# A hybrid retention and attention layer: a written order of operations in place of a list scheduler

## The chip, the core and the metric

The kernel runs on one core of one Trainium2 chip. The metric is device microseconds (us) for one execution, the median of three runs. The kernel before takes 663.64 us (663.38 to 664.61). One further execution was profiled, and its trace is what the text reads.

## What is computed

The layer works on 2048 tokens of 1024 float32 channels. All of it is float32; a dense product is made from three passes over numbers that are split into a high and a low part.

```python
def reference(x, norm_w, w_in, ret_norm_w, q_norm_w, k_norm_w, sinks, rel_bias, w_out):
    h = rms_norm(x, norm_w)                                  # 2048 x 1024
    proj = h @ w_in                                          # 2048 x 2816
    rq, rk, rv, rg, sq, sk, sv, sg = split(proj)             # 256,256,512,512,512,128,128,512
    ro = retention(rotary(rq), rotary(rk), rv)               # 4 heads, chunks of 128 tokens
    ro = groupnorm(ro) * ret_norm_w * silu(rg)
    so = sliding_window_attention(sq, sk, sv, q_norm_w, k_norm_w, sinks, rel_bias)
    so = so * silu(sg)                                       # 8 heads, window of 128 tokens
    return x + concat(ro, so) @ w_out                        # 2048 x 1024
```

## The kernel before

**The dense products.** Each of four weight blocks (512, 384, 512 and 512 columns wide on TensorE, two such columns of blocks each) is multiplied by Strassen's scheme in Winograd's form: seven products in place of eight, over pairs of 128-token tiles. `weights` and `blocks` make the sums and differences on VectorE (`sum w`, `sum x`), split each operand into a high part (`hi`, a rounding copy, mostly ScalarE) and a low part (`lo`, a subtraction on VectorE), and `products` issues 12 matmuls for each product and tile pair and gathers the results in SBUF (`copy s`, `add s`, `add t`, `add r`). In the trace these matmuls are `acc<-w,x`. The blocks stand one after the other: W2 (512 wide, until 160 us), W1 (384 wide, until about 305 us), W3 (512) and W4, the output projection (512, the last 150 us).

**The small work between them.** Attention and retention stand inside W1 and W3, in small bursts of small matmuls between the dense ones:

- `turn k`: one transpose of a key tile (`m<-ident,kn`),
- `logits`: 64 small fp32 matmuls, 128 in the trace (`m<-ks,qT`), into six PSUM banks. VectorE adds the bias to them (`lg<-m,bias,nsnk`), which frees the banks,
- `values`: 72 matmuls, 144 in the trace (`m<-pT,vn`), into four banks, which ScalarE empties (`so<-m`),
- `step`: one step of the retention (`m<-qkT`, `m<-v,qk`, `m<-state,qkT`, `m<-v,sT`).

PSUM has eight banks, and all of this shares them. SBUF tiles come from 90 places of 512 columns (tag `k`) and a few others. Between stages many tiles go through DRAM (`s_dram`, `rq_dram`, `so_dram`, `planes_dram`) and back. All plain transfers are issued by one queue, SyncE's (SP in the profile), in order: one that waits for its data holds those behind it. GpSimd (POOL) issues only the 32 adding transfers (`more`).

**What sets the order.** The program is a list of 3475 operations (`Program.op`). Each has a function that issues its instructions, the tiles that it reads and writes, a rough cost for each engine that may run it, and a due time. `Program.emit` is a list scheduler that runs while the kernel is built. It keeps a clock for each engine, takes the operation that can start first (the earlier due time decides between equals), picks a free place for each new tile, and issues the operation. It has rules for TensorE's changes between kinds of matmul, for its instruction pieces (`late`, with `PIECE`, `FIRST`, `ASKED` and `LONG`) and for the SP queue. The due times are shifted by three tables of numbers (`SHIFT`, `GROUPS`, `SINGLE`). `Order.put` then binds every instruction to the one issued before it, so that no later stage of the build changes the order.

Since every operation is issued through `Engine`, all compute instructions carry one source line, L434 in the kernel before and L497 in the changed one; the text goes by the names of tiles.

Of the kernel before, what the change touches and what calls it, by code (L numbers as in the profile page):

```python
# [63 lines left out]
SHARE = {"x": 21, "raw": 70, "acc": 96, "wr": 22, "wh": 17, "att": 49, "ret": 49, "rin": 106, "gate": 20, "mix": 35, "norm": 9, "res": 73, "turned": 2, "vn": 49, "first": 5, "block": 3, "rest": 6, "split": 57}  # L64

AHEAD_OF = {"x": 5.15, "wh": 44.79, "att": 26.63}

AHEAD, SPARE, SPARED = 15.774, 5, ("raw", "wr")
# [17 lines left out]
SEM = 0.06  # L86
# [3 lines left out]
BACKLOG = 1.5  # L90

LATE = 0.7

CUTS = {"quarters": 1, "eighths": 2, "columns": 3, "bands": 4}
ENDS = {}
CHANGE, LESSER = 0.2, 0.13

PIECE, FIRST, ASKED, LONG, MORE = 256, 193, 320, 8.0, 1.0125  # L100
# [4 lines left out]
LATER, CROWD, MOST, SOONER = 2.565, 0.719, 2, 156.112  # L105
SETTLED, INSIDE = 0.8, 0.3


def change(a, b):

    return 0.0 if a == b else LESSER if 0 < a < 3 and 0 < b < 3 else CHANGE
# [30 lines left out]
class Program:  # L142
# [5 lines left out]
    def op(self, cost, go, r=(), w=(), due=0.0, table=None, label="", also=(), many=0):  # L148


        o = Op()
        due += SHIFT.get(label, 0.0)
        due = due + GROUPS.get((label, int(due // GROUP)), 0.0) + SINGLE.get(len(self.ops), 0.0)
        o.cost, o.go, o.due, o.after, o.set, o.label, o.many = cost, go, due, [], table, label, many * MORE
# [24 lines left out]
    def emit(self):  # L179
        engines = self.engines  # L180
        avail = {e: [] for e in engines}
        free = dict.fromkeys(engines, 0.0)
        port, table, bus, cut = 0.0, None, 0.0, 0
        cap = dict(CAP)
        slots = {t: [(0.0, i) for i in range(n)] for t, n in cap.items()}
        used = dict.fromkeys(SHARE, 0)
        count = len(self.ops)
        place, border, asked = 0.0, FIRST, {}

        def late(o, s, occ):  # L190

            b, wait = border, 0.0
            while b <= place + o.many:
                a = b - ASKED
                at = s + (a - place) / o.many * occ if a >= place else asked.get(b, -LONG)
                wait = max(wait, at + LONG - s - (b - place) / o.many * occ)
                b += PIECE
            return wait

        def offer(o):  # L200
            for e in o.cost:
                bisect.insort(avail[e], (o.due, o.n, o))

        for o in self.ops:
            if not o.left:
                offer(o)
        done, now = 0, 0.0
        while done < count:
            best = None
            for e, found in avail.items():  # L210
                top = None
                base = free[e]
                if e == "T" and not cut:
                    crowd = sum(o.set in CUTS and o.ready <= base for _, _, o in found[:48])
                for due, n, o in found[:48]:
                    if top is not None and top[0] <= base + 1e-9 and not e == "T":
                        break
                    occ, lat, shared = o.cost[e]
                    s = max(base, o.ready)
                    if e == "T" and o.set:  # L220
                        if cut and o.set in CUTS:
                            s = max(base, o.ready + INSIDE)
                            if change(cut, CUTS[o.set]) < CHANGE:
                                due -= SOONER
                        else:
                            s = max(base, o.ready + SETTLED)
                            if o.set in CUTS:
                                due += LATER - CROWD * min(crowd, MOST)
                    if shared and e != "Q":
                        s = max(s, port)  # L230
                    need, short, room = {}, False, 0.0
                    for b in o.new:
                        if b.ap is None:
                            need.setdefault(b.tag, []).append(b)
                    if any(due > now + AHEAD_OF.get(b.share, 1e9) for b in o.new):
                        continue
                    spare = 0
                    if e == "Q" and need:
                        if due > now + AHEAD:
                            break  # L240
                        spare = SPARE
                    for tag, bs in need.items():
                        if tag not in slots:
                            slots[tag] = [(0.0, i) for i in range(COUNTS.get(tag, SMALL))]
                        f = slots[tag]
                        if len(f) < len(bs) + (spare if tag == "k" else 0):
                            short = True
                            break
                        room = max(room, f[len(bs) - 1][0])
                        for share in {b.share for b in bs if b.share}:  # L250
                            many = used[share] + sum(b.share == share for b in bs)
                            if many > SHARE[share] - (spare if share in SPARED else 0):
                                short = True
                    if short:
                        continue
                    s, wait = max(s, room), 0.0
                    if e == "T" and border <= place + o.many:
                        s += late(o, s, occ)
                    if e == "A" and o.set and table and o.set != table:
                        wait = 1.3  # L260
                        s += 2.0
                    if top is None or s < top[0] - 1e-9 or (s < top[0] + 1e-9 and due < top[1]):
                        top = (s, due, n, o, wait, room)
                if top is not None and (best is None or top[:3] < best[0][:3]):
                    best = top, e
            if best is None:
                self.stuck(avail, used, slots)
            (s, _, _, o, wait, room), e = best
            occ, lat, shared = o.cost[e]
            free_before = free[e]  # L270
            for e2 in o.cost:
                a = avail[e2]
                a.pop(bisect.bisect_left(a, (o.due, o.n)))
# [6 lines left out]
            if e == "Q":  # L280
                occ, lat, more = o.cost[e]
                bus = max(bus, s) + occ
                free[e] = max(s + more, bus - BACKLOG)
                o.end = bus + lat
            else:
                if wait:
                    s = s - 2.0 + wait
                if e == "A" and o.set:
                    table = o.set
                free[e] = s + occ  # L290
                o.end = s + lat
                if shared:
                    port = s + occ
                if e == "T":
                    s = max(free_before, o.ready, room) if o.set else s
                    s += change(cut, CUTS.get(o.set, 0))
                    cut = ENDS.get(o.set, CUTS.get(o.set, 0))
                    s += late(o, s, occ)
                    while border <= place + o.many:
                        border += PIECE  # L300
                    a = border - ASKED
                    while a <= place + o.many:
                        asked[a + ASKED] = s + max(a - place, 0) / max(o.many, 1) * occ if a >= place else asked.get(a + ASKED, s)
                        a += PIECE
                    place += o.many
                    free[e] = s + occ
                    o.end = s + lat
            o.seen = free[e]
            if e == "T" and o.set is None:
                now = max(now, o.due)  # L310
            o.go(engines[e])
            done += 1
            if LOG is not None:
                LOG.append((e, s, free[e], o))
            for b in o.bufs:
                b.left -= 1
                b.end = max(b.end, o.end)
                if not b.left and b.tag:
                    bisect.insort(slots[b.tag], (b.end + SEM, b.slot))
                    if b.share:  # L320
# [1493 lines left out]
```

## Time and profile before

| | us |
|---|---|
| median of three runs (lowest to highest) | 663.64 (663.38 to 664.61) |
| the profiled execution, its own time | 662.82 |
| its span, first to last instruction | 661.0 |
| TensorE (PE) busy in the span | 654.1 |
| TensorE weight loads (PEld) busy | 560.3 |
| VectorE (DVE) busy | 573.0 |
| ScalarE (ACT) busy | 466.4 |

The clock granted to TensorE was full throughout. In a row of the chain of waits the first number is the start in us, the second the length, then the engine and what it worked on; "issue" is time in which an engine waited for nothing that the profile shows. In a row of the timeline the part in brackets is idle time before the row and what ended it. A busy PE is not PE at its peak, since the ends of matmuls are modelled; so the text reads pauses of TensorE from the starts of neighbouring rows.

### The profile page before, as it was taken

Reading aid. Unit: us, or ns where it says so; the run is one execution under the profiler, and the core shown is the slowest. Engines: PE = TensorE matmul, PEld = TensorE weight load, DVE = VectorE, ACT = ScalarE, POOL = GpSimd, SP = SyncE. Lnnn points to the kernel's source line nnn. Section 1 sums busy time; section 2 is a strip of 40 time slices with the busy share of each in tenths; the row PEclk is TensorE's granted clock in tenths of the full one; section 3 lists DMA queues with packets and bytes.
Section 4 is the critical chain, followed back from the end, with each engine's and each line's share of the span. In section 5 each row is a group of like instructions: output and inputs, shape, how many; then the busy total and the mean of one; then the engine's idle time right before and its main releaser. Section 6 shows DMA issues by size and latency. Waiting matters only on the chain.

```text
span 661.0 us, 16187 instructions
## 1 busy us (share of the span) xinstructions
PE 654.1 (99%) x5926; PEld 560.3 (85%) x5926; DVE 573.0 (87%) x1328; ACT 466.4 (71%) x1140; POOL 43.5 (7%) x71
## 2 busy tenths in 40 slices
PE   9999999999999999999999999999999999999997
PEld 7888888888999999998878888888888888888886
DVE  5999985988788988799997999999999999975452
ACT  6774569958698767686988889898999675544000
POOL 0000000022300000000000000000000111133320
PEclk9999999999999999999999999999999999999999
DMA  8967369999899699699988969899999989279862
GB/s 303 389 210 249 113 200 302 367 315 310 220 253 299 189 261 288 239 331 289 298 213 259 291 168 296 247 271 272 269 277 271 230 170 234 76 116 203 191 160 96
DMA packets 153568, 160.85 MB, mean 243 GB/s; under 512 B 62096, under 2 KB 96016, under 8 KB 153488
## 3 DMA queue, kind: packets, MB, share of 16 engines
q1 hardware_dynamic: 148736, 151.43, 77.8%
q0 software_dynamic: 4608, 8.39, 8.3%
q8 instruction: 46, 0.75, 0.5%
q14 instruction: 34, 0.28, 0.1%
q10 hardware_dynamic: 144, 0.00, 0.0%
HBM read 97.58 MB, written 49.61 MB: 223 GB/s over the span
## 4 chain that ended last, share of the span: by engine, by line
PE 96%; DMA 2%; issue 0%; ACT 0%; DVE 0%; SPq 0%; POOLq 0%
PE acc L434 86%; PE m L434 10%; DMA x<-s_dram 1%; DMA x<-in_xfirst 1%; DMA rq_dram<-r 0%; SPq L434 0%; ACT x L434 0%; ACT w L434 0%; DVE x L434 0%; DVE lg L434 0%; DVE t L434 0%; DVE nm L434 0%; POOLq L434 0%
## 5 line engine op out<-in xcount | busy, mean ns | idle before, releaser
L434 PE MATMUL acc<-w,x 128*128 128x512 f32 (+1 forms) x2700 | 585.3, 377 | 0.7 <-ACT x L434 0.5
L434 PEld LDWEIGHTS acc<-w,x 128*128 128x128 f32 x2700 | 493.6, 188 | 84.6 <-issue 4.1
L434 DVE TENSOR_TENSOR x<-x 128x512 fp32r<-128x512 f32 (+2 forms) x213 | 138.5, 673 | 8.5 <-ACT x L434 8.3
L434 ACT ACTIVATE x<-x 128x512 fp32r<-128x512 f32 (+1 forms) x181 | 107.8, 620 | 42.5 <-DVE x L434 18.7
L434 DVE TENSOR_TENSOR w<-w 128x512 fp32r<-128x512 f32 (+3 forms) x96 | 61.0, 656 | 3.3 <-ACT w L434 3.1
L434 DVE TENSOR_TENSOR s<-acc,s 128x512 f32<-128x512 f32 (+1 forms) x64 | 41.6, 651 | 21.0 <-PE acc L434 20.7
L434 ACT ACTIVATE lg<-lg,nm 128x160 f32<-128x160 f32 x128 | 53.1, 418 | 7.2 <-DVE nm L434 7.1
L434 DVE SCALAR_TENSOR_TENSOR w<-w,nw_sb 128x512 fp32r<-128x512 f32 (+3 forms) x72 | 50.0, 715 | 5.1 <-ACT w L434 4.7
L434 ACT ACTIVATE w<-w 128x512 fp32r<-128x512 f32 (+1 forms) x72 | 41.7, 608 | 18.0 <-PE acc L434 9.2
L434 DVE CUSTOM_DVE_ANT_0 lg<-m,bias,nsnk 128x160 f32<-128x160 f32 x128 | 40.5, 375 | 1.5 <-PE m L434 1.5
L434 DVE TENSOR_TENSOR t<-acc,t 128x512 f32<-128x512 f32 (+2 forms) x33 | 20.8, 636 | 18.5 <-PE acc L434 18.3
L434 DVE TENSOR_TENSOR r<-acc,t 128x512 f32<-128x512 f32 (+1 forms) x32 | 20.9, 652 | 16.5 <-PE acc L434 14.0
L434 POOL DMA_DIRECT2D c<-in_xtok x8 | 7.2, 1103 | 372.4 <-DVE x L434 343.4
L434 ACT ACTIVATE w<-w,nw_sb 128x512 fp32r<-128x512 f32 (+4 forms) x41 | 26.3, 674 | 3.7 <-PE acc L434 3.1
L434 ACT ACTIVATE s<-acc 128x512 f32<-128x512 f32 (+1 forms) x32 | 18.2, 570 | 14.3 <-PE acc L434 13.7
L434 DVE STREAM_TRANSPOSE pT<-lg 128x640 f32<-128x640 f32 x32 | 25.8, 823 | 0.3 <-ACT lg L434 0.3
L434 ACT ACTIVATE ro<-ro,nmu,rg 128x128 f32<-128x128 f32 x64 | 25.3, 483 | 0.1
L434 ACT ACTIVATE c<-acc 128x512 f32<-128x512 f32 (+1 forms) x32 | 18.3, 571 | 8.7 <-PE acc L434 7.7
L434 ACT ACTIVATION_READ_ACCUMULATOR lg<-lg,nm 128x1 f32 x128 | 24.3, 189 | 0.0
L434 ACT ACTIVATE x<-go 128x512 fp32r<-128x512 f32 x26 | 15.9, 626 | 10.2 <-PE acc L434 4.3
L434 DVE TENSOR_TENSOR t<-acc,s 128x512 f32<-128x512 f32 (+1 forms) x32 | 20.7, 649 | 2.6 <-PE acc L434 2.4
L434 PE MATMUL m<-pT,vn 32*64 32x128 f32 (+1 forms) x1152 | 20.6, 285 | 0.9 <-issue 0.9
(146 smaller groups left out, 594.9 us busy)
## 6 DMA issues: line engine op xcount, KB each, us to landing
x<-in_xt SPq DMA_DIRECT2D x76, 256.0 KB, 4.9
planes_dram<-apart SPq DMA_DIRECT2D x48, 256.0 KB, 3.9
x<-s_dram SPq DMA_DIRECT2D x46, 256.0 KB, 4.4
w<-in_w_in SPq DMA_DIRECT2D x40, 256.0 KB, 5.3
xk<-in_xtok SPq DMA_DIRECT2D x32, 256.0 KB, 4.1
s_dram<-x SPq DMA_DIRECT2D x23, 256.0 KB, 3.8
w<-in_w_out SPq DMA_DIRECT2D x20, 256.0 KB, 4.0
vn<-aq_dram SPq DMA_DIRECT2D x8, 576.0 KB, 5.4
```

Source lines behind the costliest of these rows:

```text
L434: return lambda *a, **k: self.order.put(op(*a, **k))
```

## The change

The scheduler goes, and with it its rules, the shares of tiles, and the three tables of shifts. In its place stand three tables: `ORDER`, the 3475 operations as numbers in the order in which they are issued; `PLACES`, the place of each new tile, in turn; and `CHOICE`, the engine of the 18 operations that two engines could run. `emit` reads them. The operations are the same, with the same instructions, the same number of places, and the same eight banks.

```diff
     def emit(self):
-        engines = self.engines
-        avail = {e: [] for e in engines}
-        free = dict.fromkeys(engines, 0.0)
...
-        done, now = 0, 0.0
-        while done < count:
-            best = None
-            for e, found in avail.items():
...
-            o.go(engines[e])
...
+        places = iter(PLACES)
+        for n in ORDER:
+            o = self.ops[n]
             for b in o.new:
                 if b.ap is None:
-                    b.slot = slots[b.tag].pop(0)[1]
-                    if b.share:
-                        used[b.share] += 1
+                    b.slot = next(places)
                     b.ap = self.alloc(b)
...
+            o.go(self.engines[CHOICE.get(n) or next(iter(o.cost))])
+
+
+ORDER = (
+    0, 1, 2, 3, 11, 378, 379, 15, 384, 18, 389, 21, 394, 13, 380, 12, 14, 399, 382, 383, 400, 115, 401, 402, 381, 403,
...
+)
+PLACES = (
+    0, 0, 1, 2, 3, 4, 5, 6, 7, 8, 9, 10, 11, 12, 1, 2, 13, 3, 4, 14, 15, 16, 17, 18, 19, 20, 21, 22, 23, 24, 25, 26,
...
+)
+CHOICE = {380: "V", 382: "A", 38: "A", 39: "V", 36: "A", 37: "V", 866: "A", 865: "A", 864: "V", 867: "A", 2189: "A", 2188: "A", 2187: "V", 2190: "A", 2912: "V", 2909: "A", 2910: "A", 2911: "A"}
```

What the tables do to the engines' own orders is seen at three places.

**TensorE in W1.** The first rows are of the kernel before, from its first logits to the first values and on to the next logits and values.

```order
L434 MATMUL m<-ks,qT 32x160 x64
L434 MATMUL acc<-w,x 128x384 x33
L434 MATMUL m<-ident,kn 128x128
L434 MATMUL acc<-w,x 128x384 x51
L434 MATMUL m<-pT,vn 64x128 x32
L434 MATMUL m<-pT,vn 64x256 x8
L434 MATMUL m<-pT,vn 64x128 x32
L434 MATMUL acc<-w,x 128x384 x21
L434 MATMUL m<-ident,kn 128x128
L434 MATMUL acc<-w,x 128x384 x24
L434 MATMUL m<-ks,qT 32x160 x64
```

The same in the changed kernel, and behind it the second values and the third logits, and the third values and the fourth logits.

```order
L497 MATMUL m<-ks,qT 32x160 x64
L497 MATMUL acc<-w,x 128x384 x36
L497 MATMUL m<-ident,kn 128x128
L497 MATMUL acc<-w,x 128x384 x30
L497 MATMUL m<-ident,kn 128x128
L497 MATMUL acc<-w,x 128x384 x54
L497 MATMUL m<-pT,vn 64x128 x32
L497 MATMUL m<-pT,vn 64x256 x8
L497 MATMUL m<-pT,vn 64x128 x32
L497 MATMUL acc<-w,x 128x384 x24
L497 MATMUL m<-ks,qT 32x160 x64
```

```order
L497 MATMUL m<-pT,vn 64x128 x32
L497 MATMUL acc<-w,x 128x384 x15
L497 MATMUL m<-ks,qT 32x160 x64
...
L497 MATMUL m<-pT,vn 64x128 x32
L497 MATMUL acc<-w,x 128x384 x12
L497 MATMUL m<-ks,qT 32x160 x64
```

Between the first logits and the first values stand 120 dense matmuls now, 84 before. From values to the next logits there were 45 before; now there are 24, and at the next two such places 15 and 12.

**VectorE and TensorE after logits.** This is the VectorE queue of the kernel before after its fifth logits, up to the bias of the first banks.

```order
L434 TENSOR_TENSOR qn<-s,fac_89 128x512
L434 SCALAR_TENSOR_TENSOR w<-w,nw_sb 128x384 x2
L434 TENSOR_TENSOR r<-acc,t 128x384
L434 SCALAR_TENSOR_TENSOR w<-w,nw_sb 128x384 x2
L434 TENSOR_TENSOR x<-x 128x512
L434 ISA lg,nm<-m,bias,nsnk 128x160
```

In the changed kernel the tightest such place is on TensorE in W3: six dense matmuls and then a key transpose, which needs a bank that the bias frees.

```order
L497 MATMUL m<-pT,vn 64x128 x32
L497 MATMUL acc<-w,x 128x512 x36
L497 MATMUL m<-ks,qT 32x160 x64
L497 MATMUL acc<-w,x 128x512 x6
L497 MATMUL m<-ident,kn 128x128
L497 MATMUL acc<-w,x 128x512 x18
```

VectorE's queue there:

```order
L497 TENSOR_TENSOR qk<-tcos,tsin 128x8x32
L497 TENSOR_TENSOR qk<-tsin,tcos 128x8x32
L497 SCALAR_TENSOR_TENSOR w<-w,nw_sb 128x512
L497 TENSOR_TENSOR x<-x 128x512
L497 ISA lg,nm<-m,bias,nsnk 128x160
```

Two weight splits, an addition from PSUM and two more splits stood between the query's scaling and the bias before. Now two rotary sums, a weight sum and one split stand ahead of it.

**SyncE at the end.** The last rows of the queue before, and then of the changed one: `out` is the result, and c, r, s and t name its four kinds of block.

```order
L434 DMA out<-s 128x512 x2
L434 DMA out<-r 128x512
L434 DMA out<-s 128x512
L434 DMA out<-r 128x512
L434 DMA out<-s 128x512
L434 DMA out<-r 128x512
L434 DMA out<-t 128x512 x7
L434 DMA out<-t 128x384
L434 DMA out<-t 128x128
```

```order
L497 DMA out<-t 128x512
L497 DMA out<-s 128x512 x2
L497 DMA out<-t 128x512
L497 DMA out<-r 128x512 x2
L497 DMA out<-t 128x512 x3
L497 DMA out<-s 128x512 x2
L497 DMA out<-t 128x512
L497 DMA out<-r 128x512
L497 DMA out<-t 128x512
L497 DMA out<-t 128x384
L497 DMA out<-t 128x128
```

The blocks of kinds r and s, which were stored as they came, are partly stored between the last t blocks now.

At the start, the changed kernel's ScalarE runs a one-element copy first (`once`), which loads its table before any data has arrived, and VectorE, not ScalarE, makes the high part of the first 256 columns of `x`.

More of the change, by code (lines that the diff above doesn't have):

```diff
@@ L151, in op @@
         o = Op()
-        due += SHIFT.get(label, 0.0)
-        due = due + GROUPS.get((label, int(due // GROUP)), 0.0) + SINGLE.get(len(self.ops), 0.0)
-        o.cost, o.go, o.due, o.after, o.set, o.label, o.many = cost, go, due, [], table, label, many * MORE
+        o.cost, o.go, o.due, o.after, o.set, o.label, o.many = cost, go, due, [], table, label, many
         o.n, o.left, o.ready, o.end, o.seen, o.by = len(self.ops), 0, 0.0, 0.0, 0.0, None
@@ L179, in emit @@
     def emit(self):
-        engines = self.engines
-        avail = {e: [] for e in engines}
-        free = dict.fromkeys(engines, 0.0)
[L183 to L206, printed above, removed]
-        done, now = 0, 0.0
-        while done < count:
-            best = None
-            for e, found in avail.items():
[L211 to L273, printed above, removed]
@@ L274, in emit @@
+        places = iter(PLACES)
+        for n in ORDER:
+            o = self.ops[n]
             for b in o.new:
                 if b.ap is None:
-                    b.slot = slots[b.tag].pop(0)[1]
-                    if b.share:
-                        used[b.share] += 1
+                    b.slot = next(places)
                     b.ap = self.alloc(b)
[L280 to L307, printed above, removed]
@@ L308, in emit @@
-            o.seen = free[e]
-            if e == "T" and o.set is None:
-                now = max(now, o.due)
-            o.go(engines[e])
[L312 to L320, printed above, removed]
-                        used[b.share] -= 1
@@ L322, in emit @@
-            for d in o.after:
-                d.left -= 1
-                same = len(d.cost) == 1 and e in d.cost and e in ("T", "A", "Q") and not o.label.startswith("load")
-                t = o.seen if same and e != "Q" else o.end + SEM
-                if e == "Q" and now > 0:
-                    t += LATE
-                if t > d.ready:
-                    d.ready, d.by = t, o
-                if not d.left:
-                    offer(d)
-        self.time = max(free.values())
-    def stuck(self, avail, used, slots):
-        lines = [f"no operation can go: {used} { {t: len(f) for t, f in slots.items()} }"]
-        for e, found in avail.items():
-            for due, _, o in found[:4]:
-                lines.append(f"{e} {due:.1f} {o.label} needs {[(b.name, b.share) for b in o.new if b.ap is None]}")
-        raise RuntimeError("\n".join(lines))
@@ L342 @@
-LOG = None
-SHIFT = {"store ": -0.52, "square qk": -0.13, "step": -2.98, "normalise": 3.92, "lo x": -0.99, "add res": 2.35, "hi w": 1.91, "turn by dma": -5.0, "turn gated": -4.54, "load turned": 3.81, "gate": -2.87, "silu": -4.4, "sum w": 0.6, "lo w": -0.18, "sum x": -3.26, "load x": -0.14, "hi x": -0.78, "qn": 4.14, "rotary": 0.48, "bias": -0.38, "exp": 1.1, "turn weights": -1.07, "load w": 0.01, "apart": -1.33, "scale w": -4.44, "state": 0.75, "add s": 0.64, "add t": 4.54, "add r": -1.77, "more": -5.0, "copy s": -0.87, "load go": 0.06, "so": 6.55, "sum qk": 0.02, "stats": 1.22, "scale first": -2}
+            o.go(self.engines[CHOICE.get(n) or next(iter(o.cost))])
```

19 lines of the change are left out of this document (1 added, 18 removed), and 231 rows, old and new, of tables (ORDER, PLACES).

## The prediction

> **What bounds the kernel now.** I read the page first, then the chain of waits in order of time, then the timeline at each place where the chain leaves TensorE.
>
> ```profile
> span 661.0 us, 16187 instructions
> PE 654.1 (99%) x5926; PEld 560.3 (85%) x5926; DVE 573.0 (87%) x1328; ACT 466.4 (71%) x1140; POOL 43.5 (7%) x71
> ...
> PE 96%; DMA 2%; issue 0%; ACT 0%; DVE 0%; SPq 0%; POOLq 0%
> ```
>
> TensorE bounds it: 96% of the chain. The change leaves TensorE's matmuls as they are, so it can win only the time in which TensorE pauses, and the chain shows how little that is. In each of its rows stand the start, the length and the work.
>
> ```profile
> 1.68 4.08 DMA x<-in_xfirst
> ...
> 6.25 155.35 PE acc L434 x688
> 161.60 0.11 PE m L434
> ...
> 191.14 2.24 PE m L434 x124
> 193.38 0.89 issue
> 194.27 0.48 PE m L434 x15
> ...
> 216.87 2.46 PE m L434 x138
> 219.33 3.32 PE acc L434 x18
> ...
> 225.37 2.33 PE m L434 x128
> ...
> 239.46 2.57 PE m L434 x139
> ...
> 255.60 10.60 PE acc L434 x60
> ...
> 294.12 2.46 PE m L434 x138
> ...
> 482.05 43.55 PE acc L434 x192
> ...
> 526.04 131.30 PE acc L434 x588
> ...
> 657.37 0.29 DVE t L434
> ```
>
> The paces are the unit of all that follows. A 512-wide matmul takes 43.55 / 192 = 0.227 us and a 384-wide one 10.60 / 60 = 0.177 us (0.174 without its share of a changeover). A key transpose adds 0.11 us, logits 2.33 us, values 2.46 us. What the order decides is four pauses.
>
> *The hole in the second burst, 193.38.* These values took 2.24 + 0.89 + 0.48 = 3.61 us, against 2.46 us at 294.12: 1.15 us lost, with no semaphore behind it ("issue"). The transfers in that stretch, 191.0 to 193.4 us, hold this row, which the stretch of the same queue before it, 185 to 191 us, does not have:
>
> ```profile
> q8 instruction: 1, 0.02, 3.4%
> ```
>
> For the whole run the page has 46 such packets, 0.75 MB:
>
> ```profile
> q8 instruction: 46, 0.75, 0.5%
> ```
>
> TensorE's two rows count 2 x 5926 = 11852 instructions, so a packet is 11852 / 46, some 256 of them, 16 KB. One packet of instructions came while the burst was running, and TensorE stood until it was there. That is my reading; the profile names no cause. The logits (256 instructions with their weight loads) and the values (288) each use a whole packet or more in under 2.5 us, while 256 instructions of dense matmuls last 128 x 0.174 = 22 us.
>
> *The late bank, 282.26.*
>
> ```profile
> 277.35 2.40 PE L434 MATMUL m<-ks,qT 64*32 64x160 f32 x128
> 279.69 1.84 PE L434 MATMUL acc<-w,x 128*128 128x384 f32 x9
> 282.26 0.30 PE L434 MATMUL m<-ident,kn 128*128 128x128 f32 x1 [0.73 <-DVE nm L434]
> ```
>
> Nine matmuls and the changeover (18 took 3.32 at 219.33, so 0.19 over their pace) are 9 x 0.174 + 0.1 = 1.67 us, so the transpose was due at 281.36: 0.9 us lost. It waited for a bank that VectorE's bias frees. VectorE's rows say why the bias was late:
>
> ```profile
> 277.43 0.69 DVE L434 TENSOR_TENSOR qn<-s,fac 128x512 f32<-128x512 f32 x1 [1.50 <-DMA so_dram<-so]
> ...
> 281.42 0.38 DVE L434 CUSTOM_DVE_ANT_0 lg<-m,bias,nsnk 128x160 f32<-128x160 f32 x1
> 281.73 0.08 DVE L434 DVE_READ_ACCUMULATOR2_ANT nm<- 128x1 f32 x1
> 281.73 0.38 DVE L434 CUSTOM_DVE_ANT_0 lg<-m,bias,nsnk 128x160 f32<-128x160 f32 x1
> ```
>
> VectorE stood 1.50 us for a transfer, then worked off the six operations ahead of the bias without a gap, and began the bias 281.42 - 279.69 = 1.73 us after the logits were done. From its start to the transpose pass 282.26 - 281.42 = 0.84 us, two biases and the signal. So the place could bear 1.67 - 0.84 = 0.83 us, and 1.73 us late gave the pause of 0.9.
>
> *The late transpose pair, 337.08.* After a lone transpose the next matmul starts 0.03 us later (222.49 and 222.52 below); here it starts 0.36 us later. 0.33 us lost.
>
> ```profile
> 222.49 0.27 PE L434 MATMUL m<-ident,kn 128*128 128x128 f32 x1
> 222.52 2.85 PE L434 MATMUL acc<-w,x 128*128 128x384 f32 x15
> ...
> 337.08 0.27 PE L434 MATMUL m<-ident,kn 128*128 128x128 f32 x1
> 337.44 1.17 PE L434 MATMUL acc<-w,x 128*128 128x512 f32 x4
> ```
>
> *The opening.* TensorE's unbroken work begins at 6.25, after the transfer that lands at 1.68 + 4.08 = 5.76.
>
> **The change part by part.** Against the profiled execution, 662.82 us (span 661.0 and 1.8 around it); the median of the runs shown, 663.64, is 0.82 above it.
>
> The first three pauses are 1.15 + 0.90 + 0.33 = 2.38 us. Does the new order remove them? *The hole*: 120 dense matmuls stand between the first logits and the first values, where 84 stood, so the burst begins elsewhere within its 256 instructions; whether a hole comes is a matter of that place. Bounds: 1.15 won, or nothing. I take it as won, since the other seven values bursts before had no such row (216.87 is one of them). *The late bank*: VectorE now has rotary sums, a weight sum and one split ahead of the bias at its tightest place, not six operations behind a wait for a transfer. Bounds 0.9 won or nothing; I take it as won. *The transpose pair*: the same, 0.33.
>
> *The opening* stays: the first three transfers are issued in the same order, so the second half of `x` lands at 5.76 and TensorE runs from 6.25. The earlier table load moves this row off ScalarE's start:
>
> ```profile
> 3.35 1.28 ACT L434 ACT_TABLE_LOAD   x1 [3.35 <-DMA nw_sb<-in_nw]
> ```
>
> It could bring the first two matmuls forward, but those behind them wait for the landing. Bounds 0 to 0.4 won; I take 0.
> ```profile
> L434 ACT ACTIVATE x<-x 128x512 fp32r<-128x512 f32 (+1 forms) x181 | 107.8, 620 | 42.5 <-DVE x L434 18.7
> ...
> L434 ACT ACTIVATE w<-w,nw_sb 128x512 fp32r<-128x512 f32 (+4 forms) x41 | 26.3, 674 | 3.7 <-PE acc L434 3.1
> ```
>
> The moved engine choices (a net three copies from VectorE to ScalarE) lie under dense work and cost nothing; without that cover each is some 0.67 us, by the second of these rows. Transposes are as many as before, 0.11 us each, in two groups fewer: 0.
>
> *New waits.* Values fill four banks and logits need six of eight, so logits wait until ScalarE has copied the values out.
>
> ```profile
> 219.30 1.47 ACT L434 ACTIVATE so<-m 128x128 f32<-128x128 f32 x8 [1.85 <-PE m L434]
> 242.62 1.47 ACT L434 ACTIVATE so<-m 128x128 f32<-128x128 f32 x8 [1.18 <-PE acc L434]
> ```
>
> The copy takes 1.47 us and ends 1.44 us after the values at 219.33, 2.06 us after those of 239.46 + 2.57 = 242.03. The crowded places give it 24, 15 and 12 dense matmuls: 4.2, 2.6 and 2.1 us. At 12 the spare time is 0.0 to 0.65 us, at 15 it is 0.5 to 1.2, less a split of `x` (0.62, by the first of those rows) that stands between the two halves of the copy. So any lateness of ScalarE shows there. The same places bring 288 + 24 to 48 + 256 instructions in 7 to 9 us, more than two packets, where the tightest before had 33 matmuls between. Bounds for the three together: 0, or the hole of 1.15 and half a microsecond of waiting at each, 4.95. I take 0.4, near the lower end, since the closest bursts of the kernel before (values that end at 219.33, logits at 225.37) ran without a pause. *The six matmuls before the transpose in W3* last 6 x 0.227 = 1.36 us, less the same 0.84 from the bias to the transpose: VectorE may be 0.5 us late. Bounds 0 to the 0.9 seen at 282; I take 0.1.
>
> *The end.* SP now stores r and s blocks between the last t blocks. Behind the second t of the group of three stand s, s, t, r, t: with the last two of the group seven wide stores, 7 x 262 KB = 1.84 MB, ahead of the two narrow ones that end the run.
>
> ```profile
> GB/s 303 389 210 249 113 200 302 367 315 310 220 253 299 189 261 288 239 331 289 298 213 259 291 168 296 247 271 272 269 277 271 230 170 234 76 116 203 191 160 96
> ...
> out<-s SPq DMA_DIRECT2D x8, 256.0 KB, 4.4
> ...
> out<-t SPq DMA_DIRECT2D x7, 256.0 KB, 2.0
> ```
>
> At the best slice's 389 GB/s they take 4.7 us, at a middling 250 GB/s 7.4 us; t blocks come every 12 x 0.227 = 2.7 us, so about 7 us are there. Bounds: 0, or the 2.4 us by which a store among others lands later than one alone; I take 0.15.
>
> Sum: 662.82 - 2.38 + 0.4 + 0.1 + 0.15 = 661.1 for an execution like the profiled one; 0.82 above it, **661.9 us** for the median.
>
> [...]
>
> **The rivals.**
>
> *All clears* (0.13): the pauses go and nothing comes for them: 663.64 - 2.38 = 661.3, or 660.9 if the opening gains its 0.4. For it: between two uses by TensorE, VectorE's queue adds up to less than TensorE's stretch at the places that I summed. Against: the tight places above.
>
> *The pauses only move* (0.13): other transfers land late, VectorE is behind at another logits, and some 2.4 us come back: 663.6. For it: each pause came from a time that the order does not set, the landing of a packet or a transfer.
>
> *The hole is not the order's* (0.06): instructions are fetched in time, and what stopped TensorE at 193.38 stops it again: 663.64 - 0.9 - 0.33 + 0.4 = 662.8.
>
> *The crowded bursts starve* (0.13), the slower side: at the three places where logits follow values after 24, 15 and 12 matmuls, instruction packets come too late twice, once in each burst, 2 x 1.15 each: 663.64 - 2.38 + 6.9 = 668.2. It decides from 3.7 us in all, 1.25 at each place; below 2.4 us there is still a gain. For it: nothing before was that dense. Against: of all bursts before only one had a hole.
>
> **How the numbers follow.** The forecast has 0.55, and its own range is 660.7 to 663.0. A difference under 0.2%, 1.3 us, counts as no change, since runs of this kernel differ by about that. So 662.3 is the bound of faster: of the forecast 0.43 lie below it and 0.12 above, and all of "all clears": 0.56 faster. Of the pauses that move 0.10 are within, 0.03 slower; the hole that stays is within; 0.28 in all. Slower: 0.13 + 0.03 = 0.16. The range of 8 in 10 takes "all clears" on its low side and the moved pauses and half-starved bursts on its high side: 660.4 to 664.8.
>
> **What would show it.** In the changed kernel: no "issue" row inside the first values; no pause before a transpose with VectorE as releaser; the three pairs of values and close logits in W1 without a gap; dense work from about 6.2 us on; a last store that lands, as before, 3.3 us after the last addition. I am wrong if TensorE's work from 6.25 to its last matmul is not near 649 us (657.34 - 6.25 = 651.1 before), or if the end after it is longer than 4.5 us.

## The result, and the profile after

The changed kernel takes 660.58 us in the median (660.05 to 661.31), the kernel before 664.13 us in the runs beside it: a ratio of 0.9944, with a 95% interval of 0.9928 to 0.9959. That is 3.55 us less. The forecast was 661.9 us, 1.74 us less than the 663.64 us then known, so the sign is right and the gain is twice the one forecast. The time lies inside the range of 8 in 10, 660.4 to 664.8 us, and just below the forecast's own, 660.7 to 663.0. Two executions of later rounds, of 1097.63 and 1690.89 us, were disturbed, and the ranges below leave them out.

The two profiled executions show less than that. The span fell from 661.0 to 659.4 us, and the executions' own times from 662.82 to 661.31 us, which is 1.5 us. The first lies below all six timed runs of its kernel, the second is the longest of its six. So there are two questions: whether the 1.5 us came from the places that the prediction named, and where the other 2 us are.

The page of the changed kernel, with the span, the busy time by engine and the shares of the chain of waits:

```profile
span 659.4 us, 16114 instructions
PE 654.1 (99%) x5926; PEld 560.4 (85%) x5926; DVE 575.2 (87%) x1325; ACT 464.5 (70%) x1143; POOL 43.5 (7%) x71
...
PE 98%; DMA 1%; issue 0%; SPq 0%; ACT 0%; DVE 0%; POOLq 0%
```

Its chain of waits, each row with the start, the length and the work:

```profile
1.68 4.16 DMA x<-in_xfirst
...
6.33 160.55 PE acc L497 x718
...
199.13 2.46 PE m L497 x138
201.59 4.37 PE acc L497 x24
205.96 2.36 PE m L497 x128
...
223.06 2.81 PE acc L497 x15
...
245.78 2.29 PE acc L497 x12
248.07 2.33 PE m L497 x128
...
332.17 1.61 PE acc L497 x6
333.77 0.11 PE m L497
...
435.96 3.02 PE m L497 x118
438.98 0.59 issue
439.58 0.59 PE m L497 x10
...
656.16 0.29 DVE t L497
```

All the places of the prediction can be read here. The first values last 2.46 us without an "issue" row inside. The three crowded gaps of 24, 15 and 12 matmuls last 4.37, 2.81 and 2.29 us, as long as their matmuls, and logits follow at once. No transpose waits for VectorE, and the six matmuls before the transpose in W3 are followed by it directly. Dense work begins at 6.33 us (6.25 before), and TensorE's work from there to its last matmul takes 656.14 - 6.33 = 649.8 us (651.1 before; the prediction asked for about 649). The run ends 659.4 - 656.45 = 2.95 us after the last addition (661.0 - 657.66 = 3.34 before). One pause is new: a retention step, which else takes 3.25 us, takes 3.02 + 0.59 + 0.59 = 4.20 us, with an "issue" row inside. That is 0.95 us.

### The profile page after: what moved, and what is told of

Same layout as the page of the kernel before. It is cut to its first block, busy times and chain, and to the rows that moved or that the text cites. A ratio compares the mean times of both kernels' runs of the same rounds, so it can differ in the third digit from the quotient of the medians.

```text
span 659.4 us, 16114 instructions
## 1 busy us (share of the span) xinstructions
PE 654.1 (99%) x5926; PEld 560.4 (85%) x5926; DVE 575.2 (87%) x1325; ACT 464.5 (70%) x1143; POOL 43.5 (7%) x71
## 4 chain that ended last, share of the span: by engine, by line
PE 98%; DMA 1%; issue 0%; SPq 0%; ACT 0%; DVE 0%; POOLq 0%
PE acc L497 88%; PE m L497 10%; DMA x<-in_xfirst 1%; SPq L497 0%; ACT x L497 0%; DVE t L497 0%; POOLq L497 0%
## 5 line engine op out<-in xcount | busy, mean ns | idle before, releaser
L497 DVE TENSOR_TENSOR x<-x 128x512 fp32r<-128x512 f32 (+2 forms) x213 | 139.8, 677 | 13.8 <-ACT x L497 13.6
L497 ACT ACTIVATE w<-w,nw_sb 128x512 fp32r<-128x512 f32 (+4 forms) x44 | 29.1, 674 | 8.8 <-DVE w L497 4.1
L497 ACT ACTIVATE ro<-m 64x256 f32<-64x256 f32 (+2 forms) x51 | 19.6, 390 | 6.1 <-PE m L497 5.0
```

What stands on the lines that cost most here:

```text
L497: return lambda *a, **k: self.order.put(op(*a, **k))
```

## The experiments

"The kernel before" as a table means its own order of operations and places, written into the changed kernel's ORDER and PLACES; each engine then executes the same instructions as before, and single operations can be exchanged.

**Second profiles.** Both kernels were run again without an edit.

> The kernel before, unchanged, to get a second profile of it and more times. Theory A (instructions arrive late at random places): the pause with no releaser at 193.38 (0.89 us in the chain, 1.15 us in all) is gone or stands at another place in this profile, while the two pauses before transposes (0.9 us near 282, 0.33 us near 337) are there again; the runs scatter over 2 us as before, 663.4 to 665.9, by the number of such pauses, and an execution that lies at 664.1 shows two or three of them and not one. Rival B (the order itself makes that pause): it stands at 193.4 again with the same length, and the scatter comes from somewhere else, such as the end.

Measured: 663.27 us (661.54 to 666.60, 12 runs), against 663.80 us for the kernel before beside it. The chain of this second profile of the kernel before:

```profile
193.48 1.42 issue
...
554.70 8.03 DMA go<-turned_dram
...
564.25 93.12 PE acc L434 x418
```

and from its timeline VectorE's and TensorE's rows at the place of the "late bank":

```profile
276.58 0.69 DVE L434 TENSOR_TENSOR qn<-s,fac 128x512 f32<-128x512 f32 x1
...
281.94 0.27 PE L434 MATMUL m<-ident,kn 128*128 128x128 f32 x1
```

The hole in the values stands at the same place, 0.53 us longer. So theory A was wrong that its place is chance. The pause of 0.9 us at 282 is gone: VectorE did not wait for a transfer before qn, and TensorE came 0.5 us later because of the longer hole. Instead TensorE lost some 0.6 us around 564.25, where VectorE's split of x waited for a transfer that took 8.03 us. The sum of the pauses is that of the first profile within 0.1 us (1.7 + 0.05 + 0.6 for 1.15 + 0.9 + 0.33), but only the hole is the same.

> The changed kernel, unchanged, to get a second profile and more times. Theory A (instructions arrive late at random): the pause of 0.95 us at 438.98 is gone or elsewhere, and the execution takes 660.1 to 660.7 us where it has none. Rival B (the new order makes that pause): it is at 439 again, and all executions carry it. Both expect a median near 660.6.

Measured: 660.01 us (659.66 to 661.09, 5 runs). The pause at 439 is gone, and the third crowded gap has one, in the midst of the logits:

```profile
248.11 1.51 PE m L497 x76
249.62 0.42 issue
250.04 1.28 PE m L497 x52
```

These logits take 3.21 us instead of 2.33. So the changed kernel had one hole of 0.9 us in both profiles, at two places. Both profiled executions are the longest of their series (661.31 us of 660.05 to 661.31, and 661.09 of 659.66 to 661.09), so the executions that were not profiled may have less of it; no run tells.

**The place within the packets.** 

```diff
-        for n in WARM:
+        for n in WARM[:3]:
             e.matmul(pw()[:, 0:n], zero.broadcast_to([P, P]), zero.broadcast_to([P, n]), start=True, stop=True)
+        for n in range(38):
+            e.matmul(pw()[0:32, 0:16], zero.broadcast_to([P, 32]), zero.broadcast_to([P, 16]), start=True, stop=True)
```

> The changed kernel with the matmuls on zeros at the start cut into more pieces (three of 256 columns and 38 of 16 columns instead of five), so that every later TensorE instruction stands 144 places later within the packets of 256; the same order of everything else. [...] Theory A (pauses are instructions that come late): some 3 to 5 pauses of about 1 us without a releaser, inside or near the bursts of logits and values, where there was one; 662 to 665 us, most likely 663.5. Rival B (the pauses have nothing to do with instruction packets): no new pause, and 660.6 us within 0.5.

Measured: 670.18 us (668.42 to 676.16, 6 runs), 10.2 us more than the changed kernel beside it. How long ahead of its need a packet is asked for no run shows, so the number of 3 to 5 pauses was the author's estimate. The chain:

```profile
205.76 1.61 issue
...
234.51 0.69 issue
...
255.94 0.15 issue
...
259.37 1.51 issue
```

Four new pauses without a releaser stand in the bursts or right behind them. At each of them the trace has a packet of instructions that had landed 1.3 to 1.6 us before TensorE went on; at the holes of the other profiles it is 1.3 to 1.5 us. Apart from the start, nothing but the place of the instructions within their packets had been moved, so theory B falls: late instructions make these holes. Their place says the same. Counted over all of TensorE's instructions in the trace, each of the 15 such holes, in the 11 profiles of this document that have one, ends 193 instructions behind a multiple of 256: in the first profile of the kernel before after 2241 = 8 x 256 + 193, in that of the changed kernel after 9665 = 37 x 256 + 193. There the rules of the kernel before (`PIECE` 256, `FIRST` 193) let a new packet begin. From the first transpose (170.92 us here, 166.72 in the changed kernel's first profile) to that at 505 us (514.15 and 505.20) this run took 4.75 us more. The 4.2 us ahead of it were lost at the start, which I had not foreseen (see the last section).

> The kernel before with its order unchanged, and at the start six matmuls on zeros of 16 columns in place of one of 128, so that every later TensorE instruction stands 20 places later within the packets of 256. In both profiles of the kernel before, TensorE stood inside the values burst at 193.4 until 1.4 to 1.5 us after a packet of instructions had landed. Theory A (that packet makes the pause, the prediction's term of 1.15 us): the pause at 193.4 is gone or much shorter, and the median lies about 1 us below the kernel before. Rival B (something else in the order makes it): it stands where it was, within 0.3 us of its length, and the median is the same.

The edit is the same with `WARM[:4]` and `range(6)`. Measured: 662.17 us (660.42 to 665.41, 12 runs) against 662.64 us, ratio 0.9987 (0.9967 to 1.0007): by the times undecided. The timeline of its profile decides for the hole, whose values had 1.15 to 1.7 us more in every profile of the kernel before with its instructions in place:

```profile
193.13 2.53 PE L434 MATMUL m<-pT,vn 32*64 32x128 f32 x144
```

2.53 us, all in one row: the hole is gone with 20 places. This execution lost 2 us at the start again, and 0.7 us near 565.

**The pauses one by one.** First the late bank, with `1622` the two biases, `1343` the addition of r, and the rest the operations that stood between them, the splits on VectorE among them:

```diff
-    ... 1343, 928, 2184, 931, 929, 1344, 932, 1767, 1345, 1079, 1080, 1082, 1622, ...
+    ... 1343, 1622, 928, 2184, 931, 929, 1344, 932, 1767, 1345, 1079, 1080, 1082, ...
```

> The kernel before, its own order written out as a table, with one exchange: the two biases that free the bank for the key transpose at 282.26 go right behind the addition of r at 279.10 on VectorE, ahead of two splits of w and one of x. Nothing else is moved. Theory A (the term late bank of the prediction, 0.9 us, is real and can be won alone): the transpose comes at about 281.4 without a wait, and the median is 0.9 us below that of the kernel before. Rival B (pauses only move): the two splits and the split of x are 0.7 us later, TensorE waits for one of these instead, or for the later logits, and the median is within 0.3 us of the kernel before.

Measured: 664.42 us (662.85 to 666.10, 12 runs) against 663.80 us, ratio 1.0003 (0.9987 to 1.0019). Its timeline:

```profile
280.34 0.38 DVE L497 CUSTOM_DVE_ANT_0 lg<-m,bias,nsnk 128x160 f32<-128x160 f32 x1 [0.56 <-PE m L497]
...
281.83 0.27 PE L497 MATMUL m<-ident,kn 128*128 128x128 f32 x1
...
338.03 2.29 PE L497 MATMUL acc<-w,x 128*128 128x512 f32 x9 [0.68 <-DVE nm L497]
```

The bias begins right behind the logits and the transpose comes without a wait, though qn had waited 1.15 us for its transfer. But nothing is won: the pause behind the transpose near 337 is 0.9 us, where it had been 0.33. That is rival B, the pauses move.

Then all three, with the shift by 20 places, this exchange and the same for the biases at 335 (`1698` and `1700` ahead of `1731` and `2235`):

> The kernel before with all three of the prediction's pauses attacked and nothing else: the shift by 20 places, the first two biases at 282 ahead of a split of w and one of x, and the first four biases at 335 ahead of a key's rotary and a sum on VectorE. Theory A (the prediction's sum): the three pauses add up, 1.15 + 0.90 + 0.33 = 2.38 us below the kernel before, about 661.4. Theory C (in the kernel before, VectorE and ScalarE are level with TensorE at many places, so that a pause removed at one of them is met at the next, and landings that vary from run to run show up in full): less than half of it is won, 663 us or more, new waits on VectorE or on transfers stand elsewhere, and the runs still scatter over more than 2.5 us.

Measured: 664.23 us (660.74 to 665.90, 12 runs) against 662.64 us, ratio 1.0013 (0.9996 to 1.0029). The three pauses are gone. In the profile the matmul behind the transpose of W3 starts at 336.17 us, where the first profile of the kernel before has 337.44, 1.3 us earlier, though it had come 0.6 us later to its first transpose (162.08 for 161.44 us). Then it is lost:

```profile
336.17 3.68 PE L497 MATMUL acc<-w,x 128*128 128x512 f32 x15
...
429.58 10.86 PE L497 MATMUL acc<-w,x 128*128 128x512 f32 x44 [0.39 <-DVE w L497]
...
565.80 14.45 PE L497 MATMUL acc<-w,x 128*128 128x512 f32 x62 [0.83 <-DVE x L497]
```

TensorE waits for VectorE's split of w, which was not late in the profiles of the kernel before, and for the x near 565, as in the second of those profiles. That is what theory C says, and its number is met: the three edits did not win the sum of 2.38 us.

**The place near 565.** The expectation of the next run says that TensorE waited there in four of five profiles of this order; it was three. The exchange, with `2882` the store on SP:

```diff
-    2871, ... 2867, ... 3196, ... 2882, ... 3153
+    2871, 2882, ... 2867, ... 3196, ... 3153
```

> The kernel before, its own order as a table, with one exchange on SP's queue alone: the store of a piece of planes that its data let go at 535.3, and that SP issued only at 546.05 because it stood behind a load that waited for a buffer until 545.2, goes right behind the store of the piece before it, at about 540. Everything that comes of it (a transposed read, two sums and a split of x at 562.9 to 564.2, on which TensorE waited 0.6 to 1.0 us near 565 in four of five profiles of this order) is earlier by up to some us. Theory C (this chain of two transfers has no room in the kernel before, and its landings make a good part of the scatter): no wait near 565, the median 0.5 to 1.5 us below the kernel before, and the runs scatter over less than 3 us where the kernel before scattered over 5 to 6. Theory A (the three pauses of the prediction are the difference, the rest is chance): the median within 0.4 us of the kernel before, the same scatter.

Measured: 663.25 us (661.72 to 664.82, 12 runs) against 664.14 us (661.97 to 668.50, 29 runs), ratio 0.9996 (0.9981 to 1.0010). From its timeline, SP's issues and VectorE's sum:

```profile
539.58 1.05 SPq L497 DMA_DIRECT2D planes_dram<-apart  x2
...
551.01 3.25 SPq L497 DMA_DIRECT2D go<-turned_dram  x4
...
563.26 0.69 DVE L497 TENSOR_TENSOR x<-go,so 128x512 f32<-128x512 f32 x1 [0.66 <-DMA go<-turned_dram]
```

Against the second profile of the kernel before, the store goes 6 us earlier, and it doesn't help: the next link, four loads of go, is issued 0.9 us earlier and lands later. TensorE still waited there, 0.2 us, though it came 0.6 us later itself; a second late packet, in the values at 242 us, had held it 0.6 us. The runs scatter over 3.1 us, where less than 3 was expected. Theory C had the wrong link. What the loads meet there, the view of transfers shows for the stretch from 551 to 563 us (bytes of one issue and median us from issue to landing), first in this run:

```profile
out<-c SPq DMA_DIRECT2D x3, 256.0 KB, 2.8
c<-in_xtok POOLq DMA_DIRECT2D x1, 256.0 KB, 12.2
go<-turned_dram SPq DMA_DIRECT2D x4, 64.0 KB, 11.0
```

and then in the second profile of the changed kernel:

```profile
go<-turned_dram SPq DMA_DIRECT2D x4, 64.0 KB, 3.8
out<-c SPq DMA_DIRECT2D x1, 256.0 KB
```

The windows of the two (length, granted clock, share of the 16 DMA engines that is busy, above 1 where packets overlap, and GB/s), this run first and the changed kernel behind it:

```profile
557.00:560.00 3.00, 1.00 1.18 83
560.00:563.00 3.00, 1.00 1.08 276
```

```profile
557.00:560.00 3.00, 1.00 0.01 3
```

In the old order two or three stores and one or two gathers by POOL share the transfer engines with these loads, which take 6.1 to 11.0 us in four profiles of it; in the new order the engines are empty by 557 us, with a busy share of 0.00 to 0.01, and the loads take 3.6 to 3.8 us. No run moved these stores alone, so that they make the delay is read from the profiles and not shown.

All four edits together, the shift from five small matmuls behind the five wide ones:

> The kernel before with the exchange of the store and with the three edits of the run that attacked the prediction's three pauses; this time the shift by 20 places comes from five small matmuls behind the five wide ones at the start, so that the opening stays. In that earlier run TensorE was about 1.9 us ahead after the third pause and lost it again at 430 (0.56 us, VectorE's split of w) and at 565 (1.0 us). Theory C: the gain at 565 is kept now, and what was lost at 430 and later before 565 stays lost; about 661.0 us, 660.3 to 662.3, 1.5 to 3 us below the kernel before. Theory A (the sum of the prediction, 2.38 us, was reached in the chip's runs and only covered by the 565 place): 2.4 us and more below the kernel before.

Measured: 662.78 us (661.56 to 665.61, 12 runs) against 664.14 us, 1.4 us less in the medians; ratio 0.9988 (0.9969 to 1.0006). In its profile TensorE was 1.7 us ahead of the first profile of the kernel before at 336, and 0.4 us at the end. Neither theory met its number; it is nearer to C.

**Margins.** Extra work on VectorE at the same 51 places in both kernels:

```diff
+            if n in MORE:
+                for _ in range(4):
+                    self.engines["V"].memset(self.more(), 0.0)
             o.go(self.engines[CHOICE.get(n) or next(iter(o.cost))])
```

> The kernel before, its order unchanged, with extra work that nobody needs: ahead of each of 51 operations of VectorE, spread evenly over the program by number, four memsets of 128 x 64, some 0.45 us together by estimate. From the profiles of before, the time by which each of these 51 operations could be late without TensorE having to wait falls short of 0.45 us by 4.3 us in sum; for the changed kernel the same sum is 0.1 us. Theory C (the kernel before has no margin, the changed one has): 2 to 5 us slower, 666 to 669 us, with more waits on VectorE. Theory A (only the three pauses tell the kernels apart, margins don't matter): less than 1 us slower, and as much as in the changed kernel with the same extra work.

> The changed kernel with the same extra work ahead of the same 51 operations. Theory C (margins): at most 0.5 us slower than without it, 660.0 to 660.9 us, no wait of TensorE on VectorE, and runs that scatter no more than before. Theory A (margins don't matter): as much slower as the kernel before with the same work.

Measured: 681.00 us (679.36 to 683.13) for the kernel before, 18.4 us more than without; 671.95 us (670.58 to 674.15) for the changed kernel, 11 to 12 us more than its two medians without. Theory C's numbers, 2 to 5 us and at most 0.5 us, were both missed, and TensorE waits for VectorE in the changed kernel too. The memsets of one tile started 0.19 us apart, so four take 0.65 us of VectorE and not the 0.45 of the author's estimate, and by these times that is more than the changed kernel bears as well. The dose of the next two runs was chosen after this, two memsets, `range(2)`:

> The kernel before with half of the extra work on VectorE: two memsets of 128 x 64 ahead of each of the 51 operations. In the trace of the earlier run memsets start 0.19 us apart and four of them cost VectorE 0.65 us, so two cost 0.27 us. By the profiles of before, the 51 operations fall short of 0.27 us by 2.0 to 2.3 us in sum; by the profiles of the changed kernel by nothing. With four memsets both kernels lost more than twice such sums (18 us and 11 us), since lateness is carried on to the next operations. Theory C (margins): 3 to 7 us slower than the kernel before. Theory A (margins don't matter): the same loss as in the changed kernel with this work.

> The changed kernel with the same two memsets ahead of the same 51 operations. Theory C (margins): 0 to 2 us slower than without them, 660.3 to 662.3 us, at most half of what the kernel before loses by them. Theory A: as much slower as the kernel before.

Measured: 668.38 us (667.28 to 669.56, 6 runs) for the kernel before, 4.2 us more than the 664.14 us without; 661.03 us (660.10 to 662.99, 12 runs) for the changed kernel, 0.5 to 1.0 us more than its two medians without. Those are from other rounds; beside it the kernel before was 3.1 us slower, where it had been 3.55 and 3.8. The waits of TensorE (us in total, times, longest), the kernel before with the extra work:

```profile
PE acc L501 <- DVE more L501: 0.7, 1, 0.7
PE m L501 <- ACT so L501: 0.6, 1, 0.6
...
PE acc L501 <- DVE w L501: 0.5, 1, 0.5
PE m L501 <- DVE nm L501: 0.3, 1, 0.3
PE acc L501 <- DVE x L501: 0.2, 1, 0.2
```

and the changed kernel with it (the first row is the start of the program):

```profile
PE m L501 <- PEq L1869: 0.8, 1, 0.8
PE acc L501 <- ACT ro L501: 0.4, 1, 0.4
```

The same 13.8 us of work (51 x 0.27) makes TensorE wait for VectorE at four groups of places in the one kernel (the last, 0.2 us for x, stands in its second profile without the work too) and at none in the other. This is the clearest difference between the two.

Not all of the 4.2 us need be margin. TensorE's first dense rows, of the kernel before without the extra work and with it:

```profile
5.45 7.92 PE L434 MATMUL acc<-w,x 128*128 128x512 f32 x32 [0.50 <-ACT x L434]
```

```profile
5.47 7.91 PE L501 MATMUL acc<-w,x 128*128 128x512 f32 x26 [0.51 <-ACT x L501]
```

Six matmuls less in the same time are 1.4 us, lost ahead of the first memset at 39.1 us (see the last section). That execution took 668.47 us; how many of the six lost as much is not known. Without it some 3 us are left, against 0.5 to 1.0.

The traces say the same. Going back from each start on TensorE through what it needs and through the order on each engine, one can estimate by how much every VectorE operation could be later without TensorE having to wait. In the two profiles of the kernel before, 8 to 10 in 100 of these operations could not be 0.27 us late; in the two of the changed kernel, fewer than 1 in 100.

## Why the prediction was right, and too small

- *The hole, 1.15 us won.* It is gone from its place, and its cause is the one that was read from the rows: the two shifts moved and made holes with the order unchanged. But it was not won whole. The changed kernel has a hole of 0.9 us in both profiles, at 439 or at 249.6. In these two executions 0.2 to 0.3 us of the 1.15 was won.
- *The late bank, 0.90, and the transpose pair, 0.33.* Both are gone. The step that counted them as fixed prices to be added failed: in the second profile of the kernel before the first is not there and the second is 0.06 us, while 0.6 us stand near 565. What is nearly the same in the two is the sum. That each pause hides the lateness of something further on is what the single edits bear out: the pause came back near 337, at 430 and near 565.
- *The opening, 0.* Right: 6.33 for 6.25, held by the landing at 1.68 + 4.16 = 5.84.
- *The crowded gaps, 0.4.* 0 in the first profile, 0.9 in the second, at the gap of 12 matmuls. About right. The copy of so, the other suspect there, held nothing up.
- *The six matmuls in W3, 0.1, and the stores at the end, 0.15.* Neither cost anything; the end is 0.4 us shorter.
- *The sum,* 661.1 for an execution like the profiled one, met 661.31, and this is luck in part: its terms for new waits and for the end come to 0.65 us of loss, and 0.64 us was measured, but as a hole of 0.95 us at a place that it had not named, an opening 0.08 us later and an end 0.39 us shorter.
- *The step that failed* is the one that carried the sum to the median: "0.82 above it". It took the distance between the profiled execution and the median as the same in both kernels. Measured, the median lies 1.3 us above the profiled execution in the kernel before and 0.7 us below it in the changed one. That is the missing 2 us.

For the difference between executions the margin is the cause that the runs support best: a delay of 0.27 us at 51 places costs the kernel before 3 to 4.2 us and the changed kernel about 1. Landings of transfers and of instructions vary from one execution to the next (in the two profiles of the kernel before the loads of go near 551 us took 6.1 and 8.8 us in the median, and the hole 1.15 and 1.7 us), and in its profiles the kernel before lets some of this through to TensorE. Some 90 executions of it lie between 661.3 and 668.5 us; the 11 of the unedited changed kernel between 659.66 and 661.31. That the margin makes the missing 2 us is argued from this and not shown. Two other causes were seen and not set apart: a slow start, which cost 1.4 us in one of the six profiles of the old order with its start unedited and nothing in four of the changed kernel, and the hole, which the old order has in all six and twice in one. What stays open is which delays fill the longer executions of the kernel before. Its two profiled executions took 662.8 us each, and none above 664 was profiled.

Of the rivals, *the pauses only move* is what happens when the kernel before is mended at single places, but not in the changed kernel. *All clears* lay nearest in its number, at 661.3, but not in its mechanism, since a new hole came. *The crowded bursts starve* did not come to pass, though it is near: it is what the shift by 144 places does to this order. *The hole is not the order's* is out. In the first profiles of both kernels the packets of the long dense stretches, up to 161 us and from 506 us on, landed 27.07 us and more ahead of their need; in the bursts up to 1.6 us of waiting stand in the chain for one packet.

## What to carry to other kernels

Before summing up pauses on the bound engine, work out by how much the engines behind it could be late; where that is near zero, a pause removed can be met again some places further on, as here at 430 (0.39 us) and 565 (0.83 us). Take a second profile of the same kernel before pricing pauses, and count as fixed only those that stand in both. To learn whether an order has margin, put the same small extra work into both orders, in a dose near the margin that the trace shows.

## What the runs showed of the hardware

*Packets of instructions were late in bursts.* TensorE went on 1.2 to 1.6 us after the landing of the packet that it stood for, in every such hole (1.39 us in the first profile of the kernel before, 1.26 in that of the changed one). In these two profiles the transfer of a packet, 16384 bytes, took 0.88 to 2.11 us. Counted in steps of 256 from the places of the holes, the transfers of the first 45 of 46 packets started 52 to 297 instructions ahead of the need, and landed 1.26 to 32.7 us ahead of it. Moving all instructions by 20 places within the packets took one hole away, by 144 places it made four.

*TensorE's pace at the start.* The start of the run shifted by 144 places cost 4.2 us where I expected nothing. TensorE's first dense rows, of the changed kernel shifted by 144 places, of the kernel before shifted by 20, and of the kernel before in its second profile:

```profile
7.78 5.55 PE L497 MATMUL acc<-w,x 128*128 128x512 f32 x13
```

```profile
5.44 6.91 PE L434 MATMUL acc<-w,x 128*128 128x512 f32 x20 [0.15 <-ACT x L434]
```

```profile
5.33 6.99 PE L434 MATMUL acc<-w,x 128*128 128x512 f32 x27 [0.38 <-ACT x L434]
```

In the first, dense work begins 1.5 us later than in the changed kernel, and 13 matmuls take 5.55 us, 0.427 each, not 0.227; the full pace begins at 12.6 us. In the second it begins at 9.9, in the third at 6.7, and seven matmuls less in the same time are 1.6 us. The same was seen once with the start unedited (full pace from 9.4, in the kernel before with two memsets), and not in the run with three edits, whose start is cut as in the second row (full pace from 6.6). So it varies by itself, and that the cut makes it is not shown. The granted clock in the profile is 1.00 all the while, as in this row of the run shifted by 20 (start and end, length, TensorE's busy time, granted clock, DMA share, GB/s):

```profile
6.00:9.00 3.00, 3.00 (x8) 1.00 1.04 363
```

What sets the slower pace no run shows.
